# Three fused blocks on one core: fixed emission order at the block boundaries, staggered weight tiles, filler products, and narrower work in the gated-delta heads

## The chip, the cores and the metric

The kernel runs on one core of a Trainium2 chip. The metric is the device time of one execution in microseconds (us); lower is better. Before the change three runs took 3481.93, 3488.02 and 3492.93 us (median 3488.02).

## The reference, cut to what matters

The input `x` holds 512 tokens of 2048 features, float32. Three blocks follow each other, each a normalisation, an input projection, two mixers, a gate and an output projection:

```
block 1  h = rms_norm(x, gain);  z = h @ w_in                      # 8192 columns
         y = [hgrn2 (8 heads) | dilated attention (16 heads)] * silu(gates)
         x = rms_norm(x + y @ w_out, final_gain)
block 2  mod = silu(c) @ w_ada + b;  h = layernorm(x) * (1 + scale) + shift
         y = [spatial gating (8 groups) | neighbourhood attention (16 heads)]
         x = layernorm(ALPHA * x + (1 + gate) * (y @ w_out), ln_g, ln_b)
block 3  mod likewise;  h = rms_norm(x, gain) * (1 + scale) + shift
         y_gdn = gated delta rule (8 heads, chunks of 64), y_swa = window attention with a bias row per head
         x = x + gate * ((sigmoid(gl_a) * y_gdn @ wbg + sigmoid(gl_b) * y_swa @ wbs) @ w_out)
```

In a gated-delta head, `L = strict_lower(k_beta k^T * decay)` of each chunk is inverted as `(I + L)^-1`; `k_beta` is `k` times a scalar per token, and `decay` is the exponential of a difference of cumulated log-decays.

## The kernel before, in words

Activations are kept transposed, features on the 128 partitions and the 512 tokens along the row, so that a matrix of 2048 features is 16 tiles of 128x512. A product with float32 accuracy is made of three fp32r products: weights and activations are split into a rounded part `hi` and a rest `lo` (`split`, `wchunk`), and `hi*hi`, `hi*lo` and `lo*hi` are summed in one PSUM bank. A *unit* (`unit_steps`, L169) is 128 output columns: two weight transfers of 512 KB, for each of them two `hi` copies on ACT (L114) and two `lo` subtractions on DVE (L117), and 16 times 3 products of 128x512 into a bank `pm`. There are 266 units. All other products (transposes, attention, recurrences, statistics) are fp32 into banks `x`; each of them is recorded as two instructions.

Inside a block a driver (`drive`, L217) interleaves the generators of the heads with the units: each quarter unit lets every active head do its next step. Underneath, a planner sees the whole program as a dependency graph and, by its own estimate of durations, chooses the order of the instructions on each engine and on each DMA queue, and which buffer each tile gets; so an instruction may stand before one that the program emits earlier. Weight transfers, inputs and stores go through SP's queue, in order.

The places that the change touches:

- `first_units` (L187): the first four units of a block are run side by side while the 16 input tiles `h` are still being made by `make(k)`. Weights come in chunks of 512 columns for all four units at once (four tile pairs of `NW` = 5), and the products run in groups of four `k`.
- The boundary after block 1 (`out1`, L618) and after block 2 (`out2`, L808): the 16 units of the output projection; after each, DVE adds the residual and centres, ACT squares, and POOL adds three (two) running sums (L597, L853) while DVE keeps the weighted ones. After the last tile one-column products with `ones` sum over partitions (`stat_end`, L599), small column operations and a power on POOL give the token's scale and shift, `bcast_cols` (L144) spreads them over partitions by products with the identity, and `make(k)` forms the next block's input from them.
- `mods` (L564) streams 192 transfers of 512 KB for the two modulations in the background, one per weight transfer of a unit (`bg`).
- `small_products` (L908): value and gate columns of block 3, 192 products with 272 columns, after the first units.
- `rel_bias` (L1279): a 16x384 table of bias rows, written from 16 partitions to a DRAM table `reld` of 16 x 128 x 384 by one transfer of 3072 KB on ACT's queue (L1290), at the start of block 2.
- `gdn_k` (L1029): per head `k` times beta and `k` times a decay on POOL (L1045, L1048), the first of these transposed by four products; the decay by four DVE scalings (L124) and four fp32 products with `later`.
- `inverse_blocks` (L1076) inverts the 32x32 diagonal blocks of two heads by 31 short DVE steps; `inverse_join` (L1120) joins them to 64 and then to 128 by two levels of products `c f`, `y e` (and `e y` at the first level), 20 fp32 products of 128x128, with two masked copies of `at` on POOL (L1128, L1129) and three 128x512 subtractions on DVE.

## Time and profile before

| | |
|---|---|
| median of three runs | 3488.02 us |
| the profiled execution's own time | 3486.6 us |
| its span, first to last instruction | 3484.9 us |
| mean granted clock of TensorE | 0.989 |
| PE busy | 3400.8 us, 98% |
| DVE / ACT / POOL busy | 2008.9 / 1273.6 / 322.9 us |
| moved by DMA | 449.39 MB, mean 129 GB/s |

A span is the time of one execution between its first and its last instruction; the device time is 1.7 us more. [...] Names such as `pm<-a,wh` give the output tile and its inputs without buffer numbers.

### The profile page before, as it was taken

To read this page: it belongs to the slowest core of one execution; us is meant where nothing else is said; L and a number is where in the kernel's file an instruction comes from. 1 tells how busy PE (TensorE), PEld (TensorE's weight loads), DVE (VectorE), ACT (ScalarE), POOL (GpSimd) and SP (SyncE) were. 2 spreads that over 40 slices of the span, in tenths; PEclk is the share of its full clock that TensorE was granted. 3 is DMA by queue.
4 is the path that set the end of the run, shared out by engine and by line. 5 is a ranking of instruction groups with operands and counts; after the bars stand their busy time and mean duration, and the time that the engine had idled before them with its cause. 6 is when DMAs were issued, how large, how long until landed. Compare 5 with 4: busy or idle time off the path is not lost.

```text
span 3484.9 us, 44515 instructions
## 1 busy us (share of the span) xinstructions
PE 3400.8 (98%) x16678; PEld 2841.0 (82%) x16678; DVE 2008.9 (58%) x3496; ACT 1273.6 (37%) x2439; POOL 322.9 (9%) x278
## 2 busy tenths in 40 slices
PE   8999999999999899999999999999999999999999
PEld 6878888888887788888888788787878888888887
DVE  8677656556767456644368767656754433344552
ACT  4222244444434222544442243232334443432331
POOL 3000000000341000101103201111110000000000
PEclk9999999999999999999999999999999999999999
DMA  6354355435564645522234233222222233324442
GB/s 219 115 169 158 129 167 177 142 131 184 199 218 134 154 161 187 172 87 91 87 102 145 91 120 91 88 90 79 81 70 79 91 102 101 128 97 145 144 142 91
DMA packets 157640, 449.39 MB, mean 129 GB/s; under 512 B 25792, under 2 KB 35824, under 8 KB 157424
## 3 DMA queue, kind: packets, MB, share of 16 engines
q1 hardware_dynamic: 155216, 442.96, 38.5%
q10 hardware_dynamic: 2208, 3.59, 0.8%
q8 instruction: 131, 2.15, 0.3%
q14 instruction: 85, 0.70, 0.1%
HBM read 421.31 MB, written 25.17 MB: 128 GB/s over the span
## 4 chain that ended last, share of the span: by engine, by line
PE 87%; DVE 6%; issue 3%; DMA 3%; POOL 1%; ACT 1%; SPq 0%; DVEq 0%; ACTq 0%; POOLq 0%
PE pm L128 75%; PE x L128 8%; DMA gr<-in_wada_dram 2%; PE x L134 2%; PE x L527 1%; DVE wl L117 1%; DVE t L117 1%; DVE ga L120 1%; DVE fp L117 1%; DMA wr<-in_w_dram 1%; DVE t L120 1%; DVE ft L1109 0%; POOL s L142 0%; DMA t<-in_xt_dram 0%; ACT t L114 0%
## 5 line engine op out<-in xcount | busy, mean ns | idle before, releaser
L128 PE MATMUL pm<-a,wh 128*128 128x512 f32 x8512 | 2673.4, 395 | 15.2 <-ACT a L114 15.2
L128 PEld LDWEIGHTS pm<-a,wh 128*128 128x128 f32 x8512 | 1578.4, 189 | 333.3 <-ACT a L114 17.2
L128 PE MATMUL pm<-a,wl 128*128 128x512 f32 x4256 | 1668.6, 392 | 8.7 <-DVE wl L117 8.7
L117 DVE TENSOR_TENSOR wl<-wr,wh 128x512 fp32r<-128x512 f32 (+1 forms) x1080 | 764.9, 711 | 1005.3 <-ACT wh L114 940.4
L114 ACT ACTIVATE wh<-wr 128x512 fp32r<-128x512 f32 (+1 forms) x1080 | 675.9, 628 | 1767.0 <-PE pm L128 1622.6
L128 PEld LDWEIGHTS pm<-a,wl 128*128 128x128 f32 x4256 | 803.0, 189 | 182.7 <-DVE wl L117 10.5
L120 DVE SCALAR_TENSOR_TENSOR ga<-gr,sc_c,ga 128x1024 f32<-128x1024 f32 x180 | 237.8, 1321 | 78.6 <-DMA gr<-in_wada_dram 78.2
L128 PEld LDWEIGHTS x<-t,t 128*128 128x128 f32 (+2 forms) x1488 | 187.9, 188 | 31.9 <-issue 9.4
L128 PE MATMUL x<-t,t 128*128 128x64 f32 (+3 forms) x1488 | 200.6, 277 | 5.2 <-DVE t L117 4.9
L114 ACT ACTIVATE t<-x 128x512 f32<-128x512 f32 (+3 forms) x325 | 155.8, 496 | 117.5 <-PE x L128 61.3
L142 POOL TENSOR_TENSOR s<-s,nhalf 128x4 f32<-128x4 f32 (+1 forms) x51 | 60.1, 1178 | 1289.8 <-DVE s L125 1258.3
L114 ACT ACTIVATE t<-t 128x512 f32<-128x512 f32 (+1 forms) x172 | 106.8, 630 | 134.2 <-DVE t L120 83.2
L117 DVE TENSOR_TENSOR t<-t,t 128x512 f32<-128x512 f32 (+1 forms) x195 | 137.8, 707 | 23.0 <-ACT t L114 19.0
L114 ACT ACTIVATE t<-t,s 128x128 f32<-128x128 f32 (+2 forms) x192 | 98.6, 514 | 79.4 <-DVE s L438 60.2
L134 PE MATMUL x<-cst,t 128*128 128x128 f32 x496 | 74.3, 276 | 24.0 <-ACT t L114 9.8
L134 PEld LDWEIGHTS x<-cst,t 128*128 128x128 f32 x496 | 60.6, 142 | 40.0 <-ACT t L114 10.2
L597 POOL TENSOR_TENSOR acc<-acc,t 128x512 f32<-128x512 f32 x42 | 75.7, 1828 | 85.4 <-DVE t L120 71.3
L117 DVE TENSOR_TENSOR a<-t,a 128x512 fp32r<-128x512 f32 x112 | 79.3, 727 | 4.6 <-ACT a L114 4.4
L527 PE MATMUL x<-cst,t 128*128 128x128 f32 x464 | 74.5, 275 | 4.6 <-ACT t L114 4.6
L748 POOL TENSOR_TENSOR t<-cst,t 128x256 f32<-128x256 f32 x48 | 41.2, 891 | 351.7 <-DMA t<-in_rpb_dram 274.2
L114 ACT ACTIVATE t<-pm 128x512 f32<-128x512 f32 (+2 forms) x154 | 68.6, 482 | 13.5 <-PE pm L128 13.3
L120 DVE SCALAR_TENSOR_TENSOR t<-t,pm 128x512 f32<-128x512 f32 x64 | 43.7, 684 | 46.4 <-PE pm L128 46.0
(216 smaller groups left out, 1815.6 us busy)
## 6 DMA issues: line engine op xcount, KB each, us to landing
wr<-in_w_dram SPq DMA_DIRECT2D x380, 512.0 KB, 3.3
gr<-in_wada_dram SPq DMA_DIRECT2D x192, 512.0 KB, 4.2
wr<-in_wo_dram SPq DMA_DIRECT2D x96, 512.0 KB, 3.4
wr<-in_w_dram SPq DMA_DIRECT2D x48, 256.0 KB, 2.9
t<-in_xt_dram SPq DMA_DIRECT2D x32, 256.0 KB, 4.0
res<-t SPq DMA_DIRECT2D x32, 256.0 KB, 2.2
t<-res SPq DMA_DIRECT2D x32, 256.0 KB, 2.8
gld<-t SPq DMA_DIRECT2D x32, 256.0 KB, 2.0
```

The costliest lines, as they stand in the source:

```text
L114: return self.nc.scalar.activation(out, in_, fn, **kw)
L117: return self.nc.vector.tensor_tensor(out, a, b, op)
L120: return self.nc.vector.scalar_tensor_tensor(out, a, s, b, op0=op0, op1=op1)
L128: return self.nc.tensor.matmul(out, l, r, start=start, stop=stop, skip_group_check=True)
L134: self.nc.tensor.transpose(b[:, p * P:(p + 1) * P], src[:, p * P:(p + 1) * P], self.ident)
L142: self.nc.gpsimd.tensor_tensor(out, u, self.nhalf[:, :n], OP.pow)
L527: self.nc.tensor.transpose(b[:, j * P:(j + 1) * P], pr[:, j * P:(j + 1) * P], self.ident)
L597: self.nc.gpsimd.tensor_tensor(self.acc[i], self.acc[i], src, OP.add)
L748: nc.gpsimd.tensor_tensor(rows(nbs[hh][cb]), self.mask_na[:, None, v * 32:v * 32 + 32].to_broadcast([P, 8, 32]), sv[:, :, off:off + 32], O ...
```

## The change

What it does, part by part:

- **Start.** Twelve filler products with `ones` are issued first; constants are loaded later and on SP's queue; `make` of block 1 takes `hi` directly from `x` and squares on ACT, where before it made a scaled copy on ACT and squared on POOL.
- **First units.** Weight chunks are staggered: each of the four units gets its chunk of up to four `k` in another round, one chunk per round, so that one of five tile pairs is always free for the next. Round `k` makes tile `k`, finishes tile `k-1` and issues the 12 products of `k-1`; the last four `k` are issued unit by unit.
- **Boundaries.** The last unit of the projection, the statistics and the next first units are emitted inside `in_order()`, in which DVE, ACT and TensorE keep the order of the program. The sums over tiles 0 to 14 are issued inside the last unit. Fillers are put between the waits: 5, 5 and 5 after block 1; 4, 9 and 5 after block 2. The running sums of POOL go to DVE. After block 2 the three spread rows are copied to SBUF by ACT, and `small_products` is done round by round inside the first units (`side`). The row factor of block 1's output is spread only in `out2`.
- **Bias rows.** The table is made on 128 partitions (each row eight times) and written in eight transfers, each a step of the background list behind `mods`.
- **Gated-delta heads.** `kbf` is `kf` times a row of beta, read back from DRAM by one transfer per head (`beta_row`); its transposes go. `kd` moves to DVE. The decay uses two broadcast DVE operations and two fp32r products of 512 columns. The join uses a zero-padded copy of one block, writes only the changed corners, and does its second level with 64x64 weights.

```diff
+    def warm(self, n, src=None):
+        b = self.x()
+        src = self.ones if src is None else src
+        for _ in range(n):
+            self.mm(b[:, 0:src.shape[-1]], self.ones, src)
+    def in_order(self):
+        nc = self.nc
+        return self.tc.manual_schedule(engines={nc.vector.engine, nc.scalar.engine, nc.tensor.engine})
...
+        for k in range(KT + 1):                                   # first_units
+            if k and side:
+                sd = side(k - 1, rhs)
+                next(sd)
+            if k < KT:
+                next(gens[k])
+            if k:
+                next(gens[k - 1])
+                if side:
+                    next(sd)
+                rhs.append(self.end(gens[k - 1]))
+                if k < KT - 2:
+                    take(self.end(self.first_chunks(w, cts, k)))
+                if k <= KT - 4:
+                    for u in (1, 2, 3, 0):
+                        product(k - 1, u)
...
     def stat_add(self, i, k, src):
-            self.nc.gpsimd.tensor_tensor(self.acc[i], self.acc[i], src, OP.add)
+            self.tt(self.acc[i], self.acc[i], src, OP.add)
...
+    def last_unit(self, w, rhs, late):
+        steps = self.unit_steps(w, KT - 1, rhs, False)
+        for _ in range(3):
+            next(steps)
+        r = late()
+        return self.end(steps), r
...
+        last, ps = self.last_unit(self.A["wo1"], ysp, self.stat_sum)   # out1_end
+        self.warm(5, ds[0])
+        lasts = self.out1_tile(KT - 1, last, ds)
+        self.stat_last(ps, lasts)
+        self.warm(5, ds[0])
...
+        chunks = self.end(self.first_chunks(self.A["w2"], FIRST2, 0))
         gb, cb = self.bcast_cols(g), self.bcast_cols(c)
+        self.warm(5, ds[0])
...
+        last, st = self.last_unit(self.A["wo2"], ysp, late)            # out2_end
+        self.warm(4, ds[0])
+        d, sq = self.out2_tile(KT - 1, last, ds, acc, cf)
...
+        self.warm(9, ds[0])
...
+        for r, v in zip(rows, (al, be, p)):
+            b = self.bcast_cols(v)
+            self.act(r, b)
+        self.warm(5, ds[0])
...
-        for n in range(4):                                             # gdn_k
-            self.ts(gt[:, n * P:(n + 1) * P], self.triu, self.g[:, 8 * n + hd:8 * n + hd + 1])
+        gts = [self.t("w", F32R) for _ in range(2)]
+        for gt, g in zip(gts, self.ghl):
+            self.tt(gt.rearrange("p (n t) -> p n t", t=P), self.triu[:, None, :].to_broadcast([P, 4, P]),
+                    self.hc(g, hd).bitcast(F32)[:, :, None].to_broadcast([P, 4, P]))
-        self.act(kbf, self.tr4(kb))
-        for n in range(4):
-            c = slice(n * P, (n + 1) * P)
-            self.mm(gb[:, c], self.later, gt[:, c])
+        for i in range(2):
+            self.mm(gb, self.later_r, gts[i], start=i == 0, stop=i == 1)
...
+        self.tt(kbf, kf, br)
+        kd = self.y()
+        self.rows(kd, kn, self.hc(self.edl, hd))
...
+        for n in range(4):                                             # inverse_join, second level
+            self.mm(b[64:128, 64 * n:64 * n + 64], at[0:64, n * P + 64:n * P + P], f[0:64, n * P:n * P + 64])
+        self.act(y2[64:128, 0:256], b[64:128, 0:256])
...
-        nc.scalar.dma_start(self.reld, mk[0:16, None, 0:384].to_broadcast([16, P, 384]))
+        out = self.reld.rearrange("h (c j) t -> (h c) j t", j=16)
+        for j in range(0, 16, 2):
+            yield
+            nc.sync.dma_start(out[:, j:j + 2], buf[:, None, 0:384].to_broadcast([P, 2, 384]))
```

## Rows read from the trace of the kernel before

**Rows 1.** The profile page: shares of the chain of waits that ended last, by engine.
```profile
PE 87%; DVE 6%; issue 3%; DMA 3%; POOL 1%; ACT 1%; SPq 0%; DVEq 0%; ACTq 0%; POOLq 0%
```

**Rows 2.** Windows: stretch, length, busy PE, PEld, DVE, ACT, POOL, clock, DMA share, GB/s.
```profile
8.00:68.00 60.00, 52.78 (x209) 41.23 (x210) 53.07 (x73) 29.76 (x54) 26.92 (x16) 0.94 0.64 216
...
878.00:1059.40 181.40, 181.40 (x826) 150.14 (x824) 132.32 (x145) 61.64 (x105) 76.06 (x45) 1.00 0.64 217
1059.40:1080.70 21.30, 13.52 (x73) 13.05 (x71) 10.07 (x21) 4.35 (x9) 3.64 (x3) 0.68 0.30 104
1080.70:1127.70 47.00, 46.98 (x203) 38.05 (x203) 35.80 (x58) 31.18 (x50) 0.00 (x0) 0.96 0.34 113
1127.70:1190.00 62.30, 50.72 (x231) 41.66 (x230) 25.38 (x68) 11.75 (x21) 3.02 (x3) 0.92 0.65 123
...
1969.00:1989.60 20.60, 13.22 (x82) 12.98 (x80) 9.14 (x29) 3.38 (x6) 3.08 (x4) 0.66 0.11 37
1989.60:2063.00 73.40, 71.23 (x385) 60.72 (x386) 51.86 (x90) 38.00 (x71) 0.00 (x0) 0.98 0.32 103
...
2080.00:2680.00 600.00, 577.04 (x3031) 486.46 (x3030) 385.74 (x803) 199.86 (x368) 78.56 (x86) 0.99 0.26 83
```

**Rows 3.** The ending chain, its longest piece: start, length, what.
```profile
3306.69 174.13 PE pm L128 x768
```

**Rows 4.** Timeline of TensorE, first units of block 1: start, length, instruction, idle before.
```profile
43.23 0.50 PE L128 MATMUL pm<-a,wl 128*128 128x512 f32 x1 [4.12 <-DVE wl L117]
```

**Rows 5.** Timeline of the boundary after block 1.
```profile
1059.35 2.80 PE L128 MATMUL x<-ones,acc 128*128 128x1 f32 x24
1065.53 5.28 PE L128 MATMUL x<-ones,t 128*128 128x1 f32 x24 [3.38 <-DVE t L120]
1072.63 5.49 PE L128 MATMUL x<-cst,s 128*128 128x128 f32 x24 [1.81 <-POOL s L652]
1080.72 1.89 PE L128 MATMUL pm<-a,wh 128*128 128x512 f32 x5 [2.61 <-ACT a L114]
```

**Rows 6.** Timeline, a product with `ones` of 512 columns, and what follows it.
```profile
895.33 1.03 PE L128 MATMUL x<-t,ones 128*128 128x512 f32 x2
```

**Rows 7.** Timeline of the bias rows at the start of block 2.
```profile
1146.09 22.10 SPq L156 DMA_DIRECT2D wr<-in_w_dram  x5
1166.65 1.11 PE L134 MATMUL x<-cst,t 128*128 128x128 f32 x4 [9.81 <-ACT t L114]
```

**Rows 8.** Timeline of the boundary after block 2.
```profile
1982.66 4.50 PE L128 MATMUL x<-cst,s 128*128 128x128 f32 x24 [4.97 <-DVE s L117]
1989.57 2.50 PE L128 MATMUL pm<-a,wh 128*128 128x512 f32 x5 [2.41 <-ACT a L114]
```

**Rows 9.** Groups by form: busy us, mean ns, idle before; small products, and narrow weight loads.
```profile
L128 PE MATMUL pm<-wh,a 128*128 128x272 f32 x128 | 24.1, 288 | 0.0
...
L128 PEld LDWEIGHTS x<-t,t 128*128 128x128 f32 x1264 | 173.4, 192 | 24.3 <-issue 5.5 <-DVE t L120 1.3 <-ACT t L114 1.0
...
L128 PEld LDWEIGHTS x<-t,t 128*64 128x64 f32 x112 | 6.8, 140 | 4.7 <-issue 1.1
```

**Rows 10.** Timeline of TensorE in one head of the gated-delta stage.
```profile
2108.75 1.03 PE L134 MATMUL x<-cst,t 128*128 128x128 f32 x8
2109.62 1.06 PE L128 MATMUL x<-t,cst 128*128 128x128 f32 x8
```

**Rows 11.** One group of DVE in block 3, and a piece of its timeline.
```profile
L124 DVE TENSOR_SCALAR t<-cst,gx 128x128 f32<-128x128 f32 x32 | 19.5, 662 | 0.0
...
2149.63 1.16 DVE L124 TENSOR_SCALAR t<-cst,gx 128x128 f32<-128x128 f32 x1
2149.65 1.05 POOL L1045 TENSOR_TENSOR t<-t,beta 128x512 f32<-128x512 f32 x1 [0.80 <-DVE t L117]
...
2151.79 0.28 DVE L124 TENSOR_SCALAR t<-cst,gx 128x128 f32<-128x128 f32 x1
```

**Rows 12.** DMA issues: transfers, KB each, median us from issue to landing.
```profile
t<-reld SPq DMA_DIRECT2D x16, 128.0 KB, 2.5
```

## The prediction

> **What bounds the kernel now.** I read the chain of waits first: TensorE holds 87% of it [rows 1], so what counts is what TensorE does and where it does nothing. Next the spacing of its products: 768 fp32r products of 512 columns in 174.13 us are 0.2267 us each [rows 3], with no wait between them. Then the windows by stage [rows 2]: most of the kernel runs like that, and its time is the count of products. A change can gain only by taking products away, or in the stretches where PE busy is short or the clock is under 1.00. These are: the first units (7.2 us of 60 idle, clock 0.94), the boundary after block 1 (7.8 of 21.3 idle, clock 0.68), the start of block 2 (11.6 of 62.3 idle, clock 0.92), the boundary after block 2 (7.4 of 20.6 idle, clock 0.66), the stretch behind it (2.2 idle, 0.98) and the gated-delta stage (23 us of 600 idle). The change touches all of them. The running sums that move from POOL to DVE fall into the projections, whose products are the cover: PE is busy for all of 181.4 us there while DVE is busy for 132.3 [rows 2]. Three adds of about 0.7 us per tile make 32 us more for DVE, and it stays below PE; without that cover they would cost these 32 us.

> **Part by part.** The sum is made against the profiled execution's own 3486.6 us, 1.4 under the median of the runs.

> *Start.* The four first units are 192 products, 192 x 0.2267 = 43.5 us, and 16 narrow ones for the row factor, about 1.8 us at 0.112 (8 in 0.87 between the two starts of [rows 10]). They begin at 8.0 and end at 68.0: 14.7 us too long. The idle 7.2 us are mainly two waits for a weight's `lo` part on DVE, the longer of 4.12 us [rows 4]; the rest is the lower clock. In the change one chunk comes per round of 12 products (2.72 us), and a round asks three 512-column operations of DVE and three of ACT, under 2.2 us each. Bounds: nothing gained (the planner still orders this stage) to all 14.7. I leave 4 us of loss, since the first products wait for the same transfers and may find the clock low again: **gain 10.7**. The 12 fillers run before any input has landed, and cost nothing; if the cover were gone they would cost some 5 us at the low clock.

> *After block 1.* Before: 21.4 us from the last product of the projection (1059.35) to the first of block 2 (1080.72) [rows 5], and about 1.9 us more behind it, as a clock of 0.96 over 47 us [rows 2] means 3.8 us at half speed. Together 23.3. After: the 24 one-column instructions over tiles 0 to 14 move into the last unit, 2.8 us as now; then 5 fillers, the last 24 (2.8), 5 fillers, 16 instructions that spread two rows (1.8), 5 fillers. A filler is two instructions; the nearest row is the one product of that size, 0.46 us between its start and the next start, 1.03 with its drain [rows 6]. By the fp32 instructions of 128 columns, 4 x 0.112 x 2 = 0.9. I take 0.86. So 2.8 + 4.3 + 2.8 + 4.3 + 1.8 + 4.3 = 20.3. The waits under them are shorter than the fillers: from the last sum to the spread the old kernel needed about 1.8 us [rows 5]. The fillers thus set the end, and much of what the order gives they take back: 3.0, less the 8 spreading instructions that reappear in the next projection (0.9): **gain 2.1**. Bounds: fillers at half the clock, 13 more, to fillers at 0.46, 6 less.

> *Bias rows.* While the one transfer of 3072 KB runs, weight transfers queue up (22.10 us for five issues), and TensorE waits 9.81 us [rows 7]; the stretch is idle for 11.6 us and has a clock of 0.92 [rows 2], another 2 us. In the change the table leaves in eight pieces of 384 KB, one per weight transfer, after the modulations, where the weights leave the queue time. **Gain 12.5**; if each piece held the weights up by 1 us, 8 less.

> *After block 2.* Before: 20.6 us, and 73.4 for 192 products and 192 small ones (43.5 + 24.1 [rows 9] = 67.6), so 5.8 more: 26.4. After: 40 sums in the last unit (4.5), 4 fillers (3.4), 16 sums (1.8), 9 fillers (7.7), 24 spreads (2.7), 5 fillers (4.3): 24.4. The longest wait, 4.97 us for the column operations [rows 8], lies under 7.7 us of fillers. **Gain 2.0**, bounds as after block 1. In the new rounds DVE has about six operations (4 us) for 4.2 us of products: no loss, but no reserve.

> *Gated-delta heads.* Certain: four transposes of `kb` (0.43) and eight decay products (0.9, now 2 x 0.2267) go per head [rows 10]: 0.43 + 0.45 = 0.88, times 8 is 7.0. The join keeps 40 instructions per head; 24 of them get 64 columns in place of 128. A one-column instruction takes 2.80/24 = 0.117 [rows 5], so fewer moving columns alone give nothing. For the 16 with 64-column weights, weight loads of that width last 140 ns where those of 128 columns last 192 [rows 9]: 0 to 0.27 x 16 x 0.112 x 8 = 3.9; I take 2, the middle, as the weights are also shorter in rows than in any row here. DVE: four scalings of 0.662 become two broadcasts of about 0.69; `kbf` and `kd` add two; three subtractions become corners, roughly 1 us less per head. POOL loses four long operations per head, and beside one of them a scaling took 1.16 us that takes 0.28 alone [rows 11]. So some of the 23 us of idle time, in which products wait for DVE, should go: bounds -5 (the added wait for the beta row) to 12, I take 4. **Gain 13**.

> [...]

> The added wait: `kbf` on DVE waits for `beta_row`, and behind it stand the `lo` subtractions that the units' products need. Such transfers landed in 2.5 us [rows 12], and the row is asked for two driver steps (5.4 us) before its use. I cost it at nothing; it costs if SP's queue, in order, holds it behind weight transfers that wait for a buffer.

> Sum: 10.7 + 2.1 + 12.5 + 2.0 + 13 = 40.3, so 3486.6 - 40.3 = **3446 us**.

> **Rivals.**
> 1. *The fixed order turns on itself.* In `in_order` nothing can fill a late operation's place, and the fillers are paid always. For it: DVE has no reserve in the rounds after either boundary (about 2.7 of 2.72 us after block 1), and the clock was at 0.68 while one-column products ran. Against it: inputs of both stages are ready in SBUF. If each boundary loses 8 us rather than gaining 2, the time is 3466. Chance 0.18.
> 2. *DVE's bursts dissolve.* With POOL off its back and fewer operations DVE keeps up, 12 of the 23 us go, a shorter join and start give a few more: 40 + 8 + 4 = 52 off, about 3434 (the join's upper bound adds 2, the start's 2 of the 4 us left to it). For it: 1.16 against 0.28 us. Against it: the 31 steps of the inverse stay. Chance 0.22.
> 3. *Slower: the beta row.* At one place per head, the `kbf` multiply stands at DVE's head until the row lands. Weight issues before took up to 22 us for five [rows 7]. Each head whose row is late by t stalls the products by about t: it decides from 40/8 = 5 us per head; at 7 us, 3486.6 - 40 + 56 = 3503. Against it: in that stage DMA is lightly used, and one weight transfer leaves about every 5.4 us. Chance 0.04.
> 4. *The edit does not take where the planner rules.* The start keeps its stalls and the heads' idle time stays: 25 us off, 3461. Chance 0.12.

> **How the numbers follow.** My forecast, with its own range of 3439 to 3456, has 0.44. Rival 2 reaches below to some 3422, rivals 1 and 4 above to 3470; 3422 to 3470 leaves out the slower case and the tails. 0.3% of 3488 is 10.5 us, about what runs of this kernel can tell from no change. Faster by more takes the forecast and rivals 1, 2 and 4 nearly whole: 0.92. Within 0.3%: 0.04, slower: 0.04.

> **What would show it.** The start: 192 products done by about 57 us. Boundaries: about 17.5 us from the last product of a projection to the first of the next block, with the clock at 1.00 and fillers back to back; a clock of 0.5 under them would be rival 1. Start of block 2: no wait near 10 us, and eight transfers of 384 KB later. Heads: `kbf` waiting for a DMA would be rival 3; idle PE well under 18 us in the stage, rival 2. The prediction is wrong if the stages that are always busy grow, or if the start still takes 60 us.

## The result, and the profile after

The changed kernel took 3461.66 us (median of four runs, 3459.73 to 3463.57), the kernel before 3484.97 beside it: ratio 0.9931, 95% interval 0.9909 to 0.9953, so 23 us less where 40 were forecast: inside the stated range of 3422 to 3470, outside the forecast's own 3439 to 3456, and nearly half of the gain missing. A second timing of the same kernel gave 0.9921 (0.9906 to 0.9936).

The windows of the changed kernel, cut where its stages begin and end (columns as in [rows 2]):

```profile
5.50:55.40 49.90, 47.07 (x208) 37.67 (x209) 41.98 (x75) 32.08 (x58) 1.09 (x1) 1.00 0.82 279
863.10:1045.30 182.20, 182.20 (x834) 151.08 (x833) 129.13 (x187) 60.04 (x99) 0.00 (x0) 1.00 0.65 214
1045.30:1062.50 17.20, 17.20 (x73) 10.21 (x71) 8.20 (x20) 5.62 (x11) 1.98 (x2) 1.00 0.29 97
1062.50:1128.00 65.50, 51.29 (x197) 36.80 (x196) 39.13 (x62) 32.14 (x50) 0.00 (x0) 0.95 0.26 81
1128.00:1783.80 655.80, 654.66 (x3260) 550.92 (x3258) 336.35 (x647) 265.15 (x572) 50.93 (x57) 1.00 0.40 134
1783.80:1966.00 182.20, 182.20 (x812) 151.10 (x812) 128.01 (x205) 49.30 (x82) 0.53 (x1) 0.98 0.38 127
1966.00:1986.00 20.00, 20.00 (x77) 11.55 (x76) 9.73 (x30) 6.71 (x14) 2.02 (x2) 0.98 0.18 60
1986.00:2058.20 72.20, 69.69 (x387) 60.56 (x386) 56.24 (x97) 36.76 (x71) 1.58 (x3) 1.00 0.33 102
2058.20:3103.90 1045.70, 1031.97 (x5257) 862.95 (x5256) 550.65 (x1204) 389.09 (x775) 53.25 (x61) 1.00 0.30 96
```

The row to see is the fourth: the first units of block 2 take 65.5 us with TensorE idle for 14.2, where before they took 47.0 and TensorE never waited. The gated-delta stage idles about as long, 13.7 us, but over 1045.7. A table by stage comes from counting the 12768 products of 512 columns into `pm` and taking the start of the same product in both profiles (us):

| from one product to the other | before | after | gain | forecast |
|---|---|---|---|---|
| up to the 193rd (first units of block 1) | 68.0 | 55.4 | 12.5 | 10.7 |
| to the 3073rd (rest of block 1) | 811.7 | 807.7 | 4.0 | 0 |
| to the 3841st (projection and boundary) | 201.1 | 199.4 | 1.7 | 2.1 |
| to the 4033rd (first units of block 2) | 47.0 | 65.5 | -18.6 | in the line above |
| to the 6529th (rest of block 2, bias rows) | 666.1 | 655.7 | 10.3 | 12.5 |
| to the 7489th (projection, boundary, first units of block 3) | 269.1 | 274.4 | -5.3 | 2.0 |
| to the 11232nd (gated-delta stage) | 1067.6 | 1045.7 | 21.9 | 13 |
| to the last (output) | 350.0 | 350.0 | 0 | 0 |

The gains add up to 26.5 us; the two profiled executions differ by 26.9, the medians by 23.3.

The boundary itself went as written. Its timeline answers to [rows 5]: the products follow each other without a wait, two instructions to a filler, and the 24 sums of the last unit stand ahead of it:

```profile
1040.08 2.73 PE L128 MATMUL x<-ones,acc 128*128 128x1 f32 x24
...
1045.55 4.45 PE L128 MATMUL x<-t,ones 128*128 128x512 f32 x10
1049.84 2.73 PE L128 MATMUL x<-ones,t 128*128 128x1 f32 x24
1052.43 4.54 PE L128 MATMUL x<-t,ones 128*128 128x512 f32 x10
1056.81 1.95 PE L128 MATMUL x<-cst,s 128*128 128x128 f32 x16
1058.59 4.46 PE L128 MATMUL x<-t,ones 128*128 128x512 f32 x10
```

Behind it something new begins. The timeline of one round of block 2's first units, TensorE, DVE and ACT:

```profile
1077.82 0.50 PE L128 MATMUL pm<-a,wh 128*128 128x512 f32 x1 [1.07 <-DVE a L117]
1081.90 0.50 PE L128 MATMUL pm<-a,wh 128*128 128x512 f32 x1 [1.02 <-DVE a L117]
...
1079.23 0.69 DVE L117 TENSOR_TENSOR wl<-wr,wh 128x512 fp32r<-128x512 f32 x1 [1.46 <-ACT wh L114]
1079.84 1.40 DVE L117 TENSOR_TENSOR t<-t,x 128x512 f32<-128x512 f32 x2
1081.16 0.69 DVE L117 TENSOR_TENSOR a<-t,a 128x512 fp32r<-128x512 f32 x1
...
1081.27 0.81 ACT L114 ACTIVATE t<-t,mod,sc 128x512 f32<-128x512 f32 x1 [2.08 <-DVE t L117]
1082.12 0.63 ACT L114 ACTIVATE a<-t 128x512 fp32r<-128x512 f32 x1
1082.66 0.62 ACT L114 ACTIVATE wh<-wr 128x512 fp32r<-128x512 f32 x1
```

Every engine waits in it, and no one is full: the round takes 4.08 us, DVE is busy for 2.6 of them, ACT for 2.0, and TensorE has products for 2.7. DVE waits for ACT's `wh`; ACT's `wh` stands behind two operations of the next input tile; these wait for DVE's two `t`; and the next two `t` stand behind DVE's `wl`. From start to start: 0.61 (`wl` to `t`) + 0.72 + 0.72 (to ACT) + 0.85 + 0.53 + 0.65 = 4.08. That is a ring in the written order.

### The profile page after: what moved, and what is told of

It reads as the page before. It is cut to its first block, busy times and chain, and to the rows that moved or that the text cites. A ratio compares the mean times of both kernels' runs of the same rounds, so it can differ in the third digit from the quotient of the medians.

```text
span 3458.0 us, 44442 instructions
## 1 busy us (share of the span) xinstructions
PE 3408.4 (99%) x16689; PEld 2827.2 (82%) x16689; DVE 1976.9 (57%) x3593; ACT 1278.8 (37%) x2459; POOL 132.8 (4%) x156
## 4 chain that ended last, share of the span: by engine, by line
PE 53%; DVE 4%; issue 1%; ACT 1%; POOL 0%; DVEq 0%; ACTq 0%; POOLq 0%
PE pm L128 46%; PE x L128 6%; DVE fp L117 1%; PE x L614 1%; PE x L134 1%; DVE wl L117 1%; DVE ft L1275 1%; DVE t L117 1%; DVE t L120 0%; ACT t L114 0%; POOL s L142 0%; ACT wh L114 0%; DVE s L1380 0%; DVE s L117 0%; DVE ex_p L120 0%
## 5 line engine op out<-in xcount | busy, mean ns | idle before, releaser
L114 ACT ACTIVATE wh<-wr 128x512 fp32r<-128x512 f32 (+2 forms) x1073 | 671.4, 627 | 1716.3 <-PE pm L128 1626.4
L117 DVE TENSOR_TENSOR wl<-wr,wh 128x512 fp32r<-128x512 f32 (+2 forms) x1073 | 740.4, 692 | 987.8 <-ACT wh L114 921.1
L128 PEld LDWEIGHTS x<-t,t 128*128 128x128 f32 (+3 forms) x1296 | 155.6, 183 | 28.5 <-issue 6.6
L114 ACT ACTIVATE t<-t 128x512 f32<-128x512 f32 (+2 forms) x204 | 125.0, 613 | 140.0 <-DVE t L117 92.7
L128 PE MATMUL x<-t,t 128*128 128x64 f32 (+5 forms) x1296 | 167.2, 273 | 5.2 <-DVE t L117 5.2
L117 DVE TENSOR_TENSOR t<-t,t 128x512 f32<-128x512 f32 (+2 forms) x233 | 155.8, 669 | 21.8 <-ACT t L114 18.4
L134 PEld LDWEIGHTS x<-cst,t 128*128 128x128 f32 x464 | 56.5, 140 | 22.2 <-DVE t L117 3.4
L128 PE MATMUL x<-acc,t 128*128 128x128 f32 (+3 forms) x336 | 72.9, 310 | 0.0
L117 DVE TENSOR_TENSOR a<-t,a 128x512 fp32r<-128x512 f32 x96 | 63.9, 686 | 9.3 <-ACT a L114 9.1
L614 PEld LDWEIGHTS x<-cst,t 128*128 128x128 f32 x464 | 56.7, 152 | 9.9 <-ACT t L114 6.1
```

The source lines that it names most:

```text
L114: return self.nc.scalar.activation(out, in_, fn, **kw)
L117: return self.nc.vector.tensor_tensor(out, a, b, op)
L128: return self.nc.tensor.matmul(out, l, r, start=start, stop=stop, skip_group_check=True)
L134: self.nc.tensor.transpose(b[:, p * P:(p + 1) * P], src[:, p * P:(p + 1) * P], self.ident)
L614: self.nc.tensor.transpose(b[:, j * P:(j + 1) * P], pr[:, j * P:(j + 1) * P], self.ident)
```

## The experiments

Ratios are to the kernel before, timed on the same chip in the same job.

**1. The ring cut.** `wh_first` starts the round's chunk one place earlier, for block 2 only:

```
+            fc = self.first_chunks(w, cts, k) if 0 < k < KT - 2 else None
+            if early and fc:
+                next(fc)                      # transfer, and wh on ACT
             if k < KT:
                 next(gens[k])
...
-                if k < KT - 2:
-                    take(self.end(self.first_chunks(w, cts, k)))
+                if fc:
+                    take(self.end(fc))
```

> The changed kernel with one order altered: in the first units after block 1 the hi copy of a round's weight chunk is issued on ACT ahead of the affine step of the next input tile, not behind that tile's rounding. The instructions are the same ones. In the changed kernel these rounds take 4.08 us each, for 2.72 us of products. Theory (a ring in the written order): the lo part of the weights on DVE waits for the hi copy on ACT, which stands behind the affine step and the rounding of the tile whose two DVE operations stand behind the last lo part; 0.61 + 0.72 + 0.72 + 0.85 + 0.53 + 0.65 = 4.08 us. With the copy first the ring is cut, 13 rounds give back up to 1.36 us each, and the stage from the first to the 193rd product of block 2 falls from 65.5 us to 46 to 50; the time falls by 15 to 18 us, to about 3445, ratio to before 0.988. Rival 1 (DVE has no room, four operations of 0.68 in a round): rounds stay at 3.5 to 4.1 us and the time moves by less than 6 us. Rival 2 (the weight chunks land late): the waits of TensorE turn into waits of ACT for a transfer, and the stage stays above 58 us.

Measured: ratio 0.9884 (0.9868 to 0.9901). The stage takes 50.8 us, 14.8 less; its window, and ACT in a round:

```profile
1070.80:1121.60 50.80, 47.98 (x199) 37.01 (x197) 37.97 (x61) 32.50 (x50) 0.00 (x0) 0.97 0.34 104
...
1078.70 0.63 ACT L114 ACTIVATE wh<-wr 128x512 fp32r<-128x512 f32 x1 [1.40 <-PE pm L128]
1079.24 0.80 ACT L114 ACTIVATE t<-t,mod,sc 128x512 f32<-128x512 f32 x1
```

The copy now waits for TensorE to give a buffer free: TensorE is the bound again. The ring is shown, and DVE's room, which rival 1 of this run denies, is there. No operation of ACT waits for a transfer, so rival 2 falls too. The stage missed the 50 us by little, since the stalls at its end stayed: four waits, 3.4 us by the spacing of the products (2.4 as the profile counts idle time).

**2. What the fillers earn.** `no_fill` drops the six calls of `warm` at the boundaries.

```
-        self.warm(5, ds[0])        # and the five others
```

> The changed kernel without the 33 filler products at the two boundaries (15 after block 1, 18 after block 2; 66 instructions of about 0.44 us, 29 us of TensorE); the twelve at the start stay. Theory (the fillers are longer than what they cover): the boundary after block 1 falls from 17.2 to 11 to 14 us and that after block 2 from 20.1 to 14 to 17; the granted clock falls to 0.5 for a stretch behind each and takes back 2 to 4 us each; the time moves by -6 to +1 us. Rival 1 (fillers are a pure cost): the clock stays and both boundaries keep all of it, -8 to -14 us. Rival 2 (fillers earn their time through the clock): the low clock reaches well into the next products, both boundaries with the 192 products behind them take longer than with fillers, +3 to +10 us.

Measured: ratio 0.9909 (0.9894 to 0.9924), which overlaps the changed kernel's interval; by the profiles 3.2 us less. Windows of both boundaries, each with the first units behind it:

```profile
1047.30:1061.10 13.80, 8.09 (x42) 7.29 (x40) 6.86 (x19) 4.17 (x9) 1.98 (x2) 0.63 0.29 97
1061.10:1129.20 68.10, 53.72 (x197) 38.58 (x197) 39.88 (x63) 33.62 (x52) 0.00 (x0) 0.90 0.25 78
1965.70:1982.50 16.80, 8.20 (x43) 7.51 (x41) 9.41 (x30) 6.19 (x13) 2.02 (x2) 0.70 0.22 73
1982.50:2056.10 73.60, 70.99 (x384) 61.50 (x385) 56.76 (x97) 37.25 (x71) 1.58 (x3) 0.98 0.33 101
```

Each boundary is 3.4 us shorter at a clock of 0.63 and 0.70, and the units behind give back 2.5 and 1.5. Waits of 1.57, 1.87 and 2.29 us take the place of 12.6 us of fillers after block 1 (from the start of a group to the next start). So the theory holds in the main: at the two boundaries the fillers cost 6.8 us, and the clock that they hold gives back 4.0. The 1.5 of block 3 lie under the 2 to 4 expected, and in the medians the difference can't be told.

**3. The bias rows.** `bias_one` puts the old `rel_bias`, one transfer at the start of block 2, into the changed kernel; `bias_before` puts the new one alone into the kernel before.

```
-        self.bgq.append(self.rel_bias())        # bias_one, with the old function in block2
+        self.bgq.append(self.rel_bias())        # bias_before, with the new function
```

> The changed kernel with the table of bias rows as before: written at the start of block 2 from 16 partitions by one transfer of 3072 KB, not in eight pieces from 128 partitions later. Theory (the one transfer holds the weights up): a wait of TensorE of 8 to 10 us comes back behind the first units of block 2, and the time grows by 9 to 13 us over that of the changed kernel, to 3471 to 3475. Rival (the wait before was the planner's doing, and the fixed order ahead of it removes it in any case): no wait over 3 us, and a growth under 4 us.

Measured: ratio 0.9933 (0.9916 to 0.9949); the rest of block 2 took 660.1 us, 4.4 more, with one wait of 2.9 us, for DVE. Neither theory as written, though the numbers lie nearer to the rival. Its transfer left at 1116.9, while the first units still ran (they ended at 1127.0), and that of before left when they were done; the undo was therefore not a clean one, and the part was put alone into the kernel before:

> The kernel before with one part of the change alone: the table of bias rows from 128 partitions in eight pieces, one per weight transfer, behind the modulations. Theory (the one transfer held the weights up at the start of block 2): the wait of 9.8 us and the low clock beside it go, the stage from the 193rd product of block 2 to its last projection falls from 666 us to 655 to 657, the time by 9 to 12 us, ratio 0.997. Rival (undoing the same part in the changed kernel cost 4.4 us in this stage, so the transfer itself accounts for no more, and the rest of the wait was the planner's order): the stage falls by 3 to 6 us only and a wait of 3 to 6 us of TensorE for ACT stays.

Measured: ratio 0.9973 (0.9963 to 0.9982). The same stretch as [rows 7] and the eight transfers:

```profile
1129.10:1190.00 60.90, 60.90 (x294) 50.87 (x293) 32.57 (x79) 16.69 (x29) 3.40 (x3) 1.00 0.33 104
...
L1297 SPq DMA_DIRECT2D reld<-relb x8: 359/450/1021, 1532.9 to 1542.9; - x8
```

No idle time and a clock of 1.00, and the stage falls from 666.1 to 653.3: 12.8 us, the forecast's 12.5. The rival falls. The part changes three things at once (128 partitions in place of 16, eight pieces in place of one, and a later time); which of them earns it was not separated.

**4. POOL beside DVE.** `pool_load` gives the changed kernel four unread POOL products per head; `pool_to_dve` moves four of the kernel before to DVE.

```
+        for cols in (self.beta, self.edl):                                   # pool_load, gdn_k
+            nc.gpsimd.tensor_tensor(v(self.t()), v(kn), self.hc(cols, hd)[:, :, None].to_broadcast([P, 4, P]), OP.mult)
+        for i in range(2):                                                   # pool_load, inverse_join
+            nc.gpsimd.tensor_tensor(v4(self.t()), v4(at), self.mask_c[:, None, i * P:(i + 1) * P].to_broadcast([P, 4, P]), OP.mult)
...
-        nc.gpsimd.tensor_tensor(v4(c1), v4(at), m(0), OP.mult)               # pool_to_dve, also c2, kb, kd
+        self.tt(v4(c1), v4(at), m(0))
```

> The changed kernel with four long products on POOL put back into each gated-delta head, as many as before (two of k, two of the masked tile); nothing reads them. Theory (POOL's long operations slowed DVE's and made the stalls): idle time of TensorE in the gated-delta stage goes from 13.7 us back to 18 to 23, DVE's operations beside them get longer, and the time grows by 4 to 9 us. Rival (the stalls went because DVE has fewer and shorter operations and the join is narrower): the idle time stays within 3 us of 13.7 and the time within 3 us.

> The kernel before with four operations per gated-delta head moved from POOL to DVE (k times beta, k times its decay, the two masked copies); every product as before. DVE gets 32 operations of about 0.69 us more, 22 us. Theory (a long operation of POOL slows DVE's beside it, 1033 ns in place of 689 in pool_load): TensorE's idle time in the stage falls from 23.7 us by 5 to 12, and the time with it, ratio 0.997. Rival (DVE is what TensorE waits for, so 22 us more for it are 5 to 20 us more idle time): the time stays or grows by up to 15 us.

Measured: `pool_load` 0.9974 (0.9965 to 0.9983), `pool_to_dve` 0.9973 (0.9964 to 0.9983). Windows of the gated-delta stage, of the kernel before, `pool_to_dve` and `pool_load`:

```profile
2062.90:3130.40 1067.50, 1043.80 (x5334) 878.94 (x5334) 565.99 (x1195) 388.90 (x765) 90.02 (x93) 0.99 0.29 92
```
```profile
2073.00:3128.40 1055.40, 1041.68 (x5335) 878.49 (x5334) 560.12 (x1229) 389.76 (x766) 50.93 (x61) 1.00 0.29 93
```
```profile
2068.60:3129.60 1061.00, 1034.92 (x5257) 862.14 (x5256) 571.41 (x1205) 389.32 (x775) 97.29 (x93) 1.00 0.30 95
```

TensorE's idle time (length less PE) is 23.7 us before and 13.7 once the four operations are on DVE, the 13.7 that the whole change has; and 26.1 when POOL is loaded again. DVE's busy time falls by 5.9 us although it gets 32 operations more, and grows by 20.8 when POOL gets 32. One place of `pool_load`, DVE and POOL:

```profile
2190.81 0.68 DVE L117 TENSOR_TENSOR wl<-wr,wh 128x512 fp32r<-128x512 f32 x1
2194.84 1.30 DVE L117 TENSOR_TENSOR wl<-wr,wh 128x512 fp32r<-128x512 f32 x1 [2.45 <-ACT wh L114]
...
2193.05 2.55 POOL L1297 TENSOR_TENSOR t<-t,cst 128x512 f32<-128x512 f32 x2
```

The same subtraction takes 0.68 us alone and 1.30 beside POOL. Over the stage, 40 two-input DVE operations of 509 to 512 columns with both inputs in SBUF overlap a 128x512 operation of POOL and last 1136 ns in the mean, the 385 others 689; with an input in PSUM it is 734 (10) against 714 (127). Over all DVE operations of the stage that overlap a 128x512 operation of POOL, the time above the median of the same operation alone adds up to 25.8 us before, 0.8 in `pool_to_dve`, 3.0 in the changed kernel and 24.2 in `pool_load`. In `pool_to_dve` alone the idle time could also have gone because the four results come sooner from DVE; in `pool_load` nothing waits for POOL's products, so there this reason is excluded (its four more tiles also take buffers, an effect that was not separated). The theory on POOL holds in both runs; in `pool_load` the effect is larger than it said (15.3 us in the stage, of which 12.4 are idle time).

**5. The join's spacing.** `wide` widens the weights of the last level's first products (64 to 128 columns) and the moving side of its second ones.

```
-            self.mm(b[64:128, 64 * n:64 * n + 64], at[0:64, n * P + 64:n * P + P], f[0:64, n * P:n * P + 64])
+            self.mm(b[:, 64 * n:64 * n + 64], at[0:64, n * P:n * P + P], f[0:64, n * P:n * P + 64])
...
-            self.mm(b[0:64, 64 * n:64 * n + 64], y2[64:128, 64 * n:64 * n + 64], e[64:128, n * P + 64:n * P + P])
+            self.mm(b[0:64, n * P:n * P + P], y2[64:128, 64 * n:64 * n + 64], e[64:128, n * P:n * P + P])
```

> The changed kernel with the last level of the join made wider in one of two ways: its first four products of a head (8 instructions) get weights of 128 columns in place of 64 and keep 64 moving columns, its second four keep weights of 64 columns and get 128 moving columns in place of 64; the results used are the same. In the changed kernel both stand 58 ns apart (weights 64, moving 64). Theory (the columns of the weights set the spacing): the first group goes to 108 to 114 ns, the second stays within 10 ns of 58; the gated-delta stage grows by 64 x 0.054 = 3.5 us. Rival (the moving columns set it): the first stays at 58, the second goes to 108 to 114, and the stage grows by the same. Second rival (either is enough): both go to 108 to 114, and the stage grows by 7.

Measured: ratio 0.9948 (0.9931 to 0.9965). Groups by form, of the changed kernel and of `wide` (64*128: weights with 64 rows and 128 columns):

```profile
L128 PE MATMUL x<-t,t 64*64 64x64 f32 x64 | 5.4, 224 | 0.0
L128 PE MATMUL x<-acc,t 64*64 64x64 f32 x48 | 4.0, 224 | 0.0
```
```profile
L128 PE MATMUL x<-t,t 64*128 64x64 f32 x64 | 8.8, 278 | 0.0
L128 PE MATMUL x<-acc,t 64*64 64x128 f32 x48 | 6.5, 275 | 0.0
```

By the starts, both groups stand 58 ns apart in the changed kernel (median) and 112 and 109 ns in `wide`; the stage grows by 4.6 us. In the spacing the second rival holds: 128 columns on either side were enough. The stage grew by less than the 7 us it asked, though the spacings of these products alone add up to 6.7 us more (9.7 to 16.4); where the other 2.1 went was not found.

**6. The ends of the first units.** `tail_spread` is `wh_first` with the products of tiles 12 and 13 issued in their rounds, and the 40 sums in three groups; `all_but_fill` is that without the boundary fillers.

```
-                if k <= KT - 4:
+                if k <= KT - 2:
...
-                        for kk in range(KT - 4, KT):
+                        for kk in range(KT - 2, KT):
```

> The kernel wh_first with two more edits. The first units' products of tiles 12 and 13 are issued as soon as their inputs are there, not with those of 14 and 15 behind the last input; and after block 2 the 40 one-column sums stand in three groups in the last unit (8 after each of two quarters, the rest after the third), not in one stretch of 4.5 us. Theory: the stalls at the end of the first units (3.4 us of waits and 3.4 us at half the clock in wh_first's block 2, 3.4 us of waits in block 3) find products to run: block 2's first units fall from 50.8 us to 46 or 47, block 3's from 72.1 to 69 to 70, the start stays within 1 us of 50.5, the last projection of block 2 loses its stretch at the low clock (181.0 to 179.5); the time falls by 5 to 9 us under wh_first, ratio to before 0.986. Rival 1: the makes of tiles 14 and 15 are what is late (three DVE operations each), so the wait only moves and the stages shrink by less than 1.5 us. Rival 2: the banks now end 1.36 us apart in place of 2.72, and the next units wait for a bank: what the stage gives back appears behind the 193rd product.

> The kernel tail_spread without the 33 filler products at the two boundaries. Theory (in no_fill each boundary fell by 3.4 us and gave back 1.5 to 2.5 us in the 192 products behind it): here the boundaries are 13.8 and 16.7 us again, and the first units of block 2, no longer held up by a ring, lose 1 to 2 us to the lower clock; the time is 2 to 5 us under tail_spread. Rival (the clock costs what the fillers cost): within 1.5 us of tail_spread.

Measured: 0.9860 (0.9847 to 0.9874) and 0.9858 (0.9843 to 0.9873), 3437.7 and 3437.3 us: both are faster than the changed kernel and than the one before. Of `tail_spread`, the first units of blocks 2 and 3:

```profile
1069.20:1115.00 45.80, 45.40 (x199) 36.23 (x197) 36.94 (x60) 31.56 (x49) 0.00 (x0) 1.00 0.34 104
1971.50:2040.00 68.50, 68.50 (x386) 60.25 (x385) 55.57 (x96) 36.16 (x69) 1.58 (x3) 1.00 0.33 102
```

Five and 3.6 us less, and nothing comes back behind them (655.8 us for the rest of block 2). Spreading the sums gained nothing to tell: 180.8 us beside 181.0 in `wh_first`. Without fillers the boundaries lose 3.7 and 3.1 us and the units behind take 1.7 and 2.8 more; in time there is no difference, which is the rival's side.

**7. The same kernel again.**

> The changed kernel once more, to see what one profile's stages are worth. The stretch from the 193rd product to the end of block 1's units took 811.7 us in the kernel before, 807.7 in the changed one and 803.6 to 813.5 in six others. Theory (it varies from run to run, with weights landing late at other places): it differs from 807.7 by 1 to 6 us, and the 4 us that the changed kernel seemed to gain there are no effect of the change. Rival (the order that the planner gives it decides): within 0.5 us of 807.7. The first units of block 2 take 65 to 68 us and the gated-delta stage 1044 to 1046 in either case.

Measured: the rest of block 1 took 812.6 us, 4.9 more than in the first profile of the identical program, the start 52.3 us in place of 50.0 from the first product, the boundary after block 1 20.6 in place of 17.2. The first units of block 2 (65.6) and the gated-delta stage (1044.8) agree within 1 us.

## Why the prediction was right, and where it failed

- *Start, 10.7.* 12.5 and, in the second profile, 10.1, with the 193rd product at 55.4 and 57.8, where "about 57" was asked. But 2.5 of them come from the first product, which starts at 5.5 in place of 8.0 and had no term; the stage itself fell from 60.0 to 50.0 and 52.3, so 10.0 and 7.7 of the 10.7. That the sum fits so well is in part luck. The stalls that are left are two waits at the first weights (1.9 and 0.8 us by the spacing). No run takes the start apart: what the chunks, the fillers and the order each give is not shown.
- *After block 1, 2.1: the step that failed.* Projection and boundary gave 1.7, and a filler costs 0.84, where 0.86 was taken. But the sum ended at the first product of block 2. The rounds behind it, whose order the change also writes, were weighed only by how busy DVE would be (2.7 of 2.72 us), as "no reserve" under rival 1, and got no term. DVE had room (in `tail_spread` the stage takes 45.8 us and DVE is busy for 36.9 of them); the rounds are slow because DVE and ACT wait for each other in a ring, and TensorE for both. Experiment 1 takes back 14.8 of the 18.6 us, and experiment 6 the rest. So rival 1, which was given 0.18, was right in its words, the fixed order turns on itself in the rounds after a boundary, and near in size: with their projections both boundaries and what follows them lost 22.2 us (18.6 + 5.3 - 1.7), where it put 16. It was wrong in the cause, since it needs no low clock and no full engine, and the ring befell one boundary, not both.
- *Bias rows, 12.5.* 12.8 alone (shown), 10.3 in the changed kernel.
- *After block 2, 2.0.* -5.3, and -3.7 in the second profile. The boundary behind the projection came as added up (20.1 us for 24.4 less the 4.5 of sums). The projection took 7.3 more: these 4.5, 0.9 for the eight spreads, and 1.9 beside a stretch of 6.8 us at half the clock (0.7 beside 3.4 us in the second profile), which had no term. And of the 5.8 us that the first units of block 3 were to give back only 1.2 came: they kept 4.5 over their products, 3.4 of it waits in the last rounds, where three inputs are made and no product is issued. `tail_spread` takes 3.6 of these (shown). The rounds themselves held as forecast: 3.9 us of DVE under 4.3 us of products.
- *Heads, 13.* 21.9 = 11.8 of PE busy and 10.0 of idle time. The idle time was costed at 4; the bound of 12 was the nearer one, and rival 2's reason, POOL off DVE's back, accounts for all 10 in the kernel before alone (shown). By the prediction's own sign, idle time well under 18 us (it is 13.7), rival 2 came true in this stage. The join was costed at 2, and `wide` shows 4.6 by the stage and 6.7 by the spacing; that leaves 7.2 or 5.1 for the 7.0 of transposes and decay, which no run shows alone.
- *Spacing in the join.* The narrow products stand 58 ns apart, against 112 with weights of twice the columns (`wide`), where my bound from the load durations of [rows 9] (140 against 192 ns) was too tight. The same run shows the other side: with 128 moving columns the narrow weights gain next to nothing, 109 ns.
- *Beta row.* No `kbf` waits for a transfer: rival 3 did not occur. Nor did rival 4: start and heads both gained.
- *Rest of block 1, 0.* The 4.0 us can't be told from the spread: the identical program took 4.9 more the next time, and nine profiles of the changed kernel and its variants lie between 803.6 and 813.5. The kernel before and its two variants stand at 811.7, 813.4 and 821.7, so a small effect isn't excluded either. Why the stalls (up to 4.1 us at one place in the second profile) come and go was not settled.

Together: 40.3 forecast; 18.6 lost in the rounds and 7.3 in block 2's end, 8.9 more from the heads, and the rest within what two profiles of one program differ. That the time lies inside the stated range is in part luck, since one miss made up for another: without the 8.9 us that the heads gave beyond their term it would have been 3470.6, just past the upper end. And the number by itself would have spoken for rival 4 (3461), whose reason did not occur.

## What to carry to other kernels

An order written by hand has to be costed as a ring: follow one round from a result back to itself through every queue, add the latencies, and compare the sum, not the busy time of an engine, with what the round must cover. Cut it by putting on each queue first what needs only data that is already there. Before a long elementwise operation is given to POOL to relieve DVE, look at DVE's durations beside it: here DVE did the work itself in less time than it lost (in `pool_to_dve` its busy time in the stage fell by 5.9 us with 32 operations more). And a stage's gain from one profile is worth as much as the same stage's spread in a second one.

## What the runs showed of the hardware

```profile
1052.60:1073.20 20.60, 20.60 (x73) 11.66 (x71) 8.50 (x20) 5.64 (x11) 1.98 (x2) 0.83 0.21 72
```

- fp32 products of 64 weight columns and 64 moving columns stood 58 ns apart in the changed kernel; with 128 columns on either side, 109 and 112 (`wide`).
